# Block inverses of two tiles and both directions in shared banks, paired scan steps, and unread matmuls in the routes

## The chip, the core and the metric

One NeuronCore of one Trainium2 chip runs the whole program. The metric is the device time of one execution in microseconds (us); less is better. The kernel before took 1251.12 us (median of three runs, 1250.53 to 1254.74). The rows below come from one profiled execution of it, which has a time of its own. Everything is f32 or a pair of fp32r numbers (a high and a low part), so that most projections are three matmuls.

## What is computed

Two blocks over 256 tokens of 1024 channels. The first block has two layers, each a mixer and an expert layer (16 experts, 32 tokens each, chosen by the experts). The first layer's mixer is a gated delta rule with four heads in both directions, over the tokens (`lat`) and 256 tokens of context, plus a pooling branch. The second block (a linear recurrence and an attention) is not touched. Of the reference, this is what the change works on:

```python
t_mat = jnp.eye(c) + jnp.where(strict, kk * decay, 0.0) * beta[..., :, None]
u = solve(t_mat, v * beta[..., None])
wk = solve(t_mat, k * (beta * jnp.exp(gam))[..., None])

def advance(s, u_c, wk_c, kd_c, cd_c):
    w = u_c - jnp.einsum('bhck,bhkv->bhcv', wk_c, s)
    return w, cd_c * s + jnp.einsum('bhck,bhcv->bhkv', kd_c, w)

def step(s, inp):
    w, s_new = advance(s, u_c, wk_c, kd_c, cd_c)
    o = qd_c @ s + qk_c @ w
...
aff = jax.nn.softmax(jnp.einsum('bnd,de->bne', h, router), axis=-1)
gate, idx = lax.top_k(aff.transpose(0, 2, 1), cap)
xg = h[bidx, idx]
hid = silu(xg @ w_gate) * (xg @ w_up)
```

## The kernel before

**The first mixer.** The 512 tokens lie in four tiles of 128: tiles 0 and 1 are the tokens, 2 and 3 the context. For each direction `dr` and tile `tt` the kernel needs the inverse of a 128x128 unit triangular matrix for each of four heads. The diagonal 32x32 blocks are solved on VectorE (`diagonal`, unit D), then `inverse` joins them to 64 and 128 with small matmuls: 32x32 (lines 774, 779, 784) and 64x64 (792, 795), all into banks named `lv`. Each small product is evicted (to `H`, `T`, or straight into the matrix) before the next level reads it. The scan steps (`step`, 804 to 852) then run per direction and tile: kS = k S, T = v - decay kS, w = inverse T, then `wd` and dS (new state), and for token tiles the outputs oi and qS. A direction's steps hang on each other through S; the two directions don't. `pairs` lists what is done side by side: (0,2) with (1,3), (0,3) with (1,2), (0,0) with (1,1), (0,1) with (1,0).

In between, the same stage computes `ada` (A0 to A4: rows of the modulation vectors of later layers, 4 x 8 matmuls of 32x512 each, from weights that are loaded for it), `zp` (Z: two halves of the gate and pool projections), and kq (C: scores). Line numbers with a 2 or 3 in the hundreds (`L353` to `L355`) are the projections' helpers.

**What sets the order.** `ORDER["mixer0"]` names the units in order; `trace` calls them one after the other, and a unit that yields is called several times (`each`). From this a scheduler makes each engine's queue, in which it may interleave neighbours; an engine works through its queue in order. PSUM tags share banks: "ps" 2, "ada" 1, "a" 3, "b" 2. Weights are loaded by SyncE's one queue, in program order, into rings of buffers; a load waits until its buffer has been read.

**After the mixer.** A tail normalises the outputs (og, oT) and the pooled part; `residual` multiplies by the output weights; its eight tiles feed `moe` through `tile_done`, which also collects the router's sums and transposes the tokens (`xtok`). Then the route: `lg` (router logits), exponentials (`aff`), a transpose (affT), four rounds of top-8 on VectorE (`cur`), positions (`pos`, posT), the one-hot matrices (`oh`), and `xg`, the gathered tokens, with which the gate and up matmuls (gu, L1122) and the down matmuls (dn, L1148) run on weight tiles wg, wu, wd. The scaled tokens `xn` (ScalarE, L1079) are needed by xg only. The call of `free` opens the ring for the expert weights of the layer.

## Time and profile before

| what | us |
|---|---|
| runs | 1251.12 median, 1250.53 to 1254.74 |
| the profiled execution's own time | 1252.43 |
| its span | 1250.7 |
| busy in the span: TensorE, VectorE, ScalarE, GpSimd | 1094.5, 629.2, 492.8, 68.6 |
| half of the first mixer that holds inverses and steps | 176 to 266 |
| layer 0: last block of expert weights has landed | 524.25 |
| layer 1: affT, posT, first xg begin | 641.58, 647.63, 648.51 |
| layer 1: the chain enters the expert weights | 670.08 |

Three kinds of rows are used. The chain of waits follows the work that ended last back through the span; the table by stretches gives each engine's busy time, the granted TensorE clock (1.00 is 2.4 GHz, 0.50 is 1.2 GHz) and the traffic between two times; the timeline lists an engine's pieces with their start and length. A plain f32 matmul stands in the trace as two instructions, an fp32r one as one, so "x8" of lv or ada are four matmuls. In a timeline a piece's end runs into the next one's start, since matmuls are pipelined; the distance from start to start is what a piece took.

### The profile page before, as it was taken

To read this page: it belongs to the slowest core of one execution; us is meant where nothing else is said; L and a number is where in the kernel's file an instruction comes from. 1 tells how busy PE (TensorE), PEld (TensorE's weight loads), DVE (VectorE), ACT (ScalarE), POOL (GpSimd) and SP (SyncE) were. 2 spreads that over 40 slices of the span, in tenths; PEclk is the share of its full clock that TensorE was granted. 3 is DMA by queue.
4 is the path that set the end of the run, shared out by engine and by line. 5 is a ranking of instruction groups with operands and counts; after the bars stand their busy time and mean duration, and the time that the engine had idled before them with its cause. 6 is when DMAs were issued, how large, how long until landed. Compare 5 with 4: busy or idle time off the path is not lost.

```text
span 1250.7 us, 19471 instructions
## 1 busy us (share of the span) xinstructions
PE 1094.5 (88%) x7728; PEld 741.0 (59%) x7728; DVE 629.2 (50%) x1442; ACT 492.8 (39%) x1035; POOL 68.6 (5%) x118
## 2 busy tenths in 40 slices
PE   5999999989799666799979956668999999999997
PEld 2667656658443120299844411117898699988875
DVE  3548972354321010378631100017887887689875
ACT  4347553243201000255511100006778466566663
POOL 0050000000000000000000000000001100011100
PEclk9999899999799777799979987878999999999999
DMA  9578565579999999998459999994352145433220
GB/s 387 201 271 307 200 265 196 173 270 374 372 422 421 421 422 421 422 420 335 160 223 416 421 421 422 421 421 188 125 187 94 68 151 183 161 136 129 102 102 34
DMA packets 48043, 339.71 MB, mean 272 GB/s; under 512 B 5328, under 2 KB 5584, under 8 KB 7248
## 3 DMA queue, kind: packets, MB, share of 16 engines
q1 hardware_dynamic: 46800, 336.38, 68.4%
q10 hardware_dynamic: 1152, 2.09, 0.5%
q8 instruction: 61, 1.00, 0.3%
q14 instruction: 30, 0.25, 0.1%
HBM read 337.40 MB, written 1.05 MB: 271 GB/s over the span
## 4 chain that ended last, share of the span: by engine, by line
PE 39%; DMA 23%; issue 7%; DVE 5%; ACT 2%; POOL 1%; POOLq 0%; DVEq 0%; SPq 0%; ACTq 0%
DMA w<-wu 8%; DMA w<-wg 8%; DMA w<-wd 6%; PE gu L1122 3%; PE xg L1097 2%; PE sc L344 2%; PE sc L342 2%; PE sc L343 2%; PE qkvg L342 2%; PE qkvg L344 2%; PE qkvg L343 2%; DMA pk<-pk 1%; PE dn L1148 1%; PE res L342 1%; PE res L343 1%
## 5 line engine op out<-in xcount | busy, mean ns | idle before, releaser
L297 DVE TENSOR_TENSOR wl<-w,wh 128x512 fp32r<-128x512 f32 x304 | 208.4, 695 | 82.8 <-ACT wh L211 72.9
L211 ACT ACTIVATE wh<-w 128x512 fp32r<-128x512 f32 x304 | 189.2, 631 | 144.9 <-PE res L343 25.8
L1122 PE MATMUL gu<-w,xg 128*32 128x512 f32 x1024 | 161.0, 729 | 50.9 <-DMA w<-wu 28.1
L1122 PEld LDWEIGHTS gu<-w,xg 128*32 128x32 f32 x1024 | 30.3, 117 | 164.8 <-DMA w<-wu 74.0
L1148 PE MATMUL dn<-w,hidT 128*32 128x512 f32 x512 | 70.4, 652 | 21.7 <-DMA w<-wd 16.1
L1137 DVE TENSOR_TENSOR hid<-hid,gu 128x512 f32<-128x512 f32 x8 | 5.5, 686 | 159.7 <-PE gu L1122 159.7
L211 ACT ACTIVATE y<-dn 128x512 f32<-128x512 f32 x16 | 9.6, 598 | 188.2 <-PE dn L1148 188.2
L232 DVE SCALAR_TENSOR_TENSOR xT<-sc,adac,xT 128x256 f32<-128x256 f32 x64 | 27.9, 480 | 106.4 <-PE sc L1156 106.4
L342 PE MATMUL qkvg<-u_f,wh 128*128 128x272 f32 (+1 forms) x256 | 74.1, 290 | 0.0
L344 PE MATMUL qkvg<-u_f,wl 128*128 128x272 f32 (+1 forms) x256 | 73.2, 286 | 0.0
L343 PE MATMUL qkvg<-u_f,wh 128*128 128x272 f32 (+1 forms) x256 | 72.8, 284 | 0.0
L437 PE MATMUL ada<-w,cs 128*32 128x512 f32 x320 | 54.6, 641 | 1.3 <-DMA w<-ada 1.3
L344 PE MATMUL sc<-hT,wl 128*128 128x258 f32 x192 | 54.7, 285 | 0.9 <-DVE wl L297 0.9
L342 PE MATMUL sc<-hT,wh 128*128 128x258 f32 x192 | 54.6, 284 | 0.2 <-DVE xT L232 0.2
L343 PE MATMUL sc<-hT,wh 128*128 128x258 f32 x192 | 54.2, 282 | 0.0
L1148 PEld LDWEIGHTS dn<-w,hidT 128*32 128x32 f32 x512 | 14.2, 115 | 66.7 <-DMA w<-wd 37.1
L342 PEld LDWEIGHTS qkvg<-u_f,wh 128*128 128x128 f32 x256 | 48.1, 188 | 3.0 <-issue 1.8
L344 PEld LDWEIGHTS qkvg<-u_f,wl 128*128 128x128 f32 x256 | 48.2, 188 | 0.8 <-issue 0.8
L343 PEld LDWEIGHTS qkvg<-u_f,wh 128*128 128x128 f32 x256 | 48.2, 188 | 0.0
L1136 ACT ACTIVATE hid<-gu 128x512 f32<-128x512 f32 x8 | 4.8, 598 | 104.4 <-PE gu L1122 104.4
L1156 PE MATMUL sc<-sg,y 128*128 128x256 f32 x128 | 37.3, 442 | 8.5 <-ACT y L211 8.4
L1156 PEld LDWEIGHTS sc<-sg,y 128*128 128x128 f32 x128 | 26.3, 216 | 25.9 <-ACT y L211 22.2
(613 smaller groups left out, 2624.8 us busy)
## 6 DMA issues: line engine op xcount, KB each, us to landing
w<-wu SPq DMA_DIRECT2D x64, 1024.0 KB, 19.8
w<-wg SPq DMA_DIRECT2D x64, 1024.0 KB, 19.8
w<-wd SPq DMA_DIRECT2D x64, 1024.0 KB, 19.8
w<-ada SPq DMA_DIRECT2D x48, 1024.0 KB, 5.3
w<-f_in SPq DMA_DIRECT2D x16, 1024.0 KB, 4.9
w<-sc_in SPq DMA_DIRECT2D x12, 1024.0 KB, 19.8
w<-e_out SPq DMA_DIRECT2D x8, 1024.0 KB, 5.3
w<-ev_ws SPq DMA_DIRECT2D x6, 1024.0 KB, 6.0
```

Of the source, the lines that this page charges most:

```text
L211: return self.nc.scalar.activation(out, in_, AF.Copy)
L232: return self.nc.vector.scalar_tensor_tensor(out, a, s, b, op0=op0, op1=op1, **kw)
L297: self.nc.vector.tensor_sub(lo, x, hi.bitcast(F32))
L342: mm(out, wh, xh, start=(kt == 0), stop=False)
L343: mm(out, wh, xl, start=False, stop=False)
L344: self.last_mm = mm(out, wl, xh, start=False, stop=(kt == nk - 1)).ins
L437: nc.tensor.matmul(a[32 * q:32 * q + 32, :], self.cs[:, kt, :], w[:, q * 512:(q + 1) * 512], start=(kt == 0), stop=(kt == KT - 1), tile_po ...
L1097: nc.tensor.matmul(a[:, :256], xn[:, i, ft * P:(ft + 1) * P], oh[:, i].rearrange("p e s -> p (e s)"), start=(i == 0), stop=(i == 1))
L1122: nc.tensor.matmul(a[32 * e:32 * e + 32, :], xg[g // 2][:, kt, s:s + 32], w[:, e * 512:(e + 1) * 512], start=(kt == 0), stop=(kt == KT - 1 ...
L1137: v.tensor_mul(hid, hid, pu[1])
L1148: nc.tensor.matmul(a[32 * e:32 * e + 32, :], hT[:, t, 32 * e:32 * e + 32], w[:, e * 512:(e + 1) * 512], start=(t == 0), stop=(t == 3), til ...
L1156: nc.tensor.matmul(a[:, j * 256:(j + 1) * 256], y[:, (2 * f2 + j) * P:(2 * f2 + j + 1) * P], sg[g // 2][:, g % 2], start=True, stop=True)
```

## The change

`inverse(n)` now treats two tiles and both directions at once: n is 0 or 1 (tiles 0 and 1, or 2 and 3), its products of both directions and tiles go into one shared bank for each level, and each eviction takes all of them (or one direction) at once. It yields four times. `step(pair, last)` runs both directions of a pair side by side, operation by operation, and yields twice: once after the state, once after the outputs. `ORDER["mixer0"]` is rewritten for these units: I0 is `inverse(1)` (context), I1 is `inverse(0)`; the gates and decays stand earlier, the ada units later. In the route, `warm(n)` adds n unread f32 matmuls of 128x256 into the "ada" bank: five behind the last `lg`, ten behind affT. The last two `xtok` transposes come behind `lg`, and the `xn` activations behind the exponentials. (`ada_columns` is split out of `ada` without effect; a new `ada_sum` is called by no unit, since ADA_SUM is empty.) In the diff the removed lines of `inverse` and `step`, which stand in the code above, are left out.

```diff
+WARM = 5, 10
+ADA_SUM = ()
...
 ORDER = {
-    "mixer0": "k0 K0 G A0 W0 A1 W1 W0 W1 W1 W1 W0 W0 k1 K1 k2 K2 k3 K3 Q0 R0 R1 R2 R3 v0 V0 v1 V1 v3 V3 v2 V2 Q1 Q2 "
-              "Q3 D A2 A3 I0 I0 I1 I0 I0 I1 U I1 P0 I2 I3 P1 I1 P0 P1 C0 Z I2 C1 P2 Z Z I2 I3 P3 I2 P2 A4 I3 Z I3 "
-              "P3",
+    "mixer0": "k0 G W1 K0 W1 W0 W0 A0 W1 W0 W1 W0 k1 K1 k2 K2 A1 k3 K3 Q0 R0 R1 R2 R3 v0 V0 v1 V1 v3 V3 v2 V2 Q1 Q2 "
+              "Q3 D A2 I0 I1 A3 I0 I0 I0 U P0 P0 I1 A4 P1 Z I1 I1 C1 C0 P1 Z P2 Z Z P2 P3 P3",
...
-        def inverse(pair):
...
+        def inverse(n):
...
+            q4 = lambda q: slice(32 * q, 32 * q + 32)
+            half = lambda i: slice(64 * i, 64 * i + 64)
+            ts = slice(2 * n, 2 * n + 2)
+            dirs = [(AA[0][:, ts], R_[:, 0, ts], RT_[:, 0, ts], 0, 1), (AA[1][:, ts], RT_[:, 1, ts], R_[:, 1, ts], 1, 0)]
+            blocks = [(p, *d, 2 * p + d[3], 2 * p + d[4]) for p in range(2) for d in dirs]
+            th = [(t, h) for t in range(2) for h in range(4)]
+            T = gw.tile([P, 2, 4, 64], F32, tag="YT64", name="YT64", bufs=1)
+            H = gw.tile([P, 2, 4, 32], F32, tag="H32", name="H32", bufs=1)
+            a, a2 = (self.ps("lv", t).rearrange("p (x t h c) -> p x t h c", x=2, t=2, h=4) for t in "ba")
+            for p, A, Yi, YT, R, C, r, c in blocks:
+                for t, h in th:
+                    mm(a[q4(c), 0, t, h], A[q4(r), t, h, q4(c)], YT[q4(r), t, h], start=True, stop=True,
+                       tile_position=(32 * r, 32 * c))
+            self.copy(H, a[:, 0], "act")
+            g.memset(T, 0.0)
+            for Z, Yi, YT, R, C in dirs:
+                for q in (2 * R, 2 * R + 1):
+                    self.copy(T[q4(q), :, :, q4(q % 2)], YT[q4(q)])
+            yield
+            for p, A, Yi, YT, R, C, r, c in blocks:
+                for t, h in th:
+                    mm(a[q4(r), 1, t, h], H[q4(c), t, h], Yi[q4(c), t, h], start=True, stop=True,
+                       tile_position=(32 * c, 32 * r))
+            for p, A, Yi, YT, R, C, r, c in blocks:
+                if p == R:
...
+            for p, Z, Yi, YT, R, C, r, c in blocks:
+                nc.scalar.activation(Z[q4(r), :, :, q4(c)], a[q4(r), 1], AF.Copy, scale=-1.0)
+                if p == R:
+                    v.tensor_scalar(T[q4(c), :, :, q4(r % 2)], a2[q4(c), 0], -1.0, None, op0=OP.mult)
+            for Z, Yi, YT, R, C in dirs:
                 for q in range(4):
...
+                    self.copy(Z[q4(q), :, :, q4(q)], Yi[q4(q)])
+            yield
+            H = gw.tile([P, 2, 4, 64], F32, tag="H64", name="H64", bufs=1)
+            b, b2 = (self.ps("lv", t).rearrange("p (t h c) -> p t h c", t=2, h=4) for t in "bb")
+            for A, _, _, R, C in dirs:
+                for t, h in th:
+                    mm(b[half(C), t, h], A[half(R), t, h, half(C)], T[half(R), t, h], start=True, stop=True,
+                       tile_position=(64 * R, 64 * C))
+            self.copy(H, b, "act")
+            yield
+            for Z, _, _, R, C in dirs:
+                for t, h in th:
+                    mm(b2[half(R), t, h], H[half(C), t, h], Z[half(C), t, h, half(C)], start=True, stop=True,
+                       tile_position=(64 * C, 64 * R))
+            for Z, _, _, R, C in dirs:
+                v.tensor_scalar(Z[half(R), :, :, half(C)], b2[half(R)], -1.0, None, op0=OP.mult)
+            yield
...
+        def step(pair, last):
...
             hd = lambda t, h: t[:, h * P:(h + 1) * P]
...
+            tk = lambda tt: slice(tt * P, (tt + 1) * P)
+            mm = lambda out, x, y: nc.tensor.matmul(out, x, y, start=True, stop=True)
+            T1, w, wr, old = {}, {}, {}, list(S)
+            for dr, tt in pair:
+                if S[dr] is None:
+                    T1[dr] = vtok[:, tt, :]
+                    continue
                 a = self.ps("kS", "a")
                 for h in range(4):
...
+                    mm(hd(a, h), kT[:, h, tk(tt)], hd(S[dr], h))
+                T1[dr] = sw.tile([P, 512], F32, tag="T1", name="T1")
                 for h in range(4):
...
+                    self.stt(hd(T1[dr], h), hd(a, h), neg[:, dr, tt, h:h + 1], hd(vtok[:, tt, :], h), OP.mult, OP.add)
+            for dr, tt in pair:
+                w[dr] = b = self.ps("w", "a")
+                for h in range(4):
+                    mm(hd(b, h), AA[dr][:, tt, h], hd(T1[dr], h))
+            wd = {}
+            for dr, tt in pair if not last else ():
+                wd[dr] = sw.tile([P, 512], F32, tag="wd", name="wd")
+                for h in range(4):
+                    nc.scalar.activation(hd(wd[dr], h), hd(w[dr], h), AF.Copy, scale=bkd[:, dr, tt, h:h + 1])
+            for dr, tt in pair if pair[0][1] < 2 else ():
+                wr[dr] = sw.tile([P, 512], F32, tag="wr", name="wr")
+                for h in range(4):
+                    nc.scalar.activation(hd(wr[dr], h), hd(w[dr], h), AF.Copy, scale=beta[:, tt, 4 * dr + h:4 * dr + h + 1])
             if not last:
...
+                for dr, tt in pair:
+                    c = self.ps("dS", "a")
                     for h in range(4):
...
+                        mm(hd(c, h), hd(ktok[:, tt, :], h), hd(wd[dr], h))
+                    Sn = sw.tile([P, 512], F32, tag=f"S{dr}", name="S")
+                    if S[dr] is None:
+                        v.tensor_copy(Sn, c)
+                    else:
+                        for h in range(4):
+                            self.stt(hd(Sn, h), hd(S[dr], h), ec[:, dr, 2, tt, h:h + 1], hd(c, h), OP.mult, OP.add)
+                    S[dr] = Sn
+            yield
+            for dr, tt in pair if pair[0][1] < 2 else ():
                 e = self.ps("oi", "a")
                 for h in range(4):
...
+                    mm(hd(e, h), KQ[dr][:, tt, h], hd(wr[dr], h))
                 f = self.ps("qS", "a")
                 for h in range(4):
...
+                    mm(hd(f, h), qT[:, h, tk(tt)], hd(old[dr], h))
                 O = oacc[tt]
                 of = O.rearrange("p h d -> p (h d)")
                 if not done[tt]:
                     v.tensor_add(of, of, e)
                 for h in range(4):
                     self.stt(O[:, h], hd(f, h), ec[:, dr, 0, tt, h:h + 1], O[:, h], OP.mult, OP.add)
...
+            yield
         pairs = [[(0, 2), (1, 3)], [(0, 3), (1, 2)], [(0, 0), (1, 1)], [(0, 1), (1, 0)]]
...
-        def steps(i):
-            for dr, tt in pairs[i]:
-                step(dr, tt, i == 3)
-                yield
...
-            units[f"I{h}"] = each(inverse(pairs[h]), 4)
-            units[f"P{h}"] = each(steps(h), 2)
+            units[f"P{h}"] = each(step(pairs[h], h == 3), 2)
...
+        for n in range(2):
+            units[f"I{n}"] = each(inverse(1 - n), 4)
...
+    def warm(self, n):
+        x = self.xT.rearrange("p k t -> p (k t)")
+        a = self.ps("warm", "ada")
+        for i in range(n):
+            self.nc.tensor.matmul(a[:, :256], self.ident, x[:, :256], start=True, stop=True)
...
+                        self.last_lg = nc.tensor.matmul(lg[:, 64 * i + 32 * n + m:][:, :m], (x, sq)[n][:, t],
+                                                        (Rs[:, kt], self.ones)[n][:, :m], start=True, stop=True).ins
+            with self.tc.issue_after(self.last_lg) if kt == KT - 1 else ExitStack():
+                for i in range(2):
+                    pe = self.tp(xt[i][kt // 4][:, (kt % 4) * P:(kt % 4 + 1) * P], x[:, i * P:(i + 1) * P])
             return pe
...
+        with self.tc.issue_after(self.last_lg):
+            self.warm(WARM[0])
...
-            nc.scalar.activation(aff[:, i], aff[:, i], AF.Exp, bias=mx[:, i:i + 1], accum_out=ex[:, i:i + 1])
+            e = nc.scalar.activation(aff[:, i], aff[:, i], AF.Exp, bias=mx[:, i:i + 1], accum_out=ex[:, i:i + 1])
...
         for i in range(2):
-            self.tp(at[:16, i * P:(i + 1) * P], aff[:, i])
+            at_ins = self.tp(at[:16, i * P:(i + 1) * P], aff[:, i]).ins
+        with self.tc.issue_after(at_ins):
+            self.warm(WARM[1])
...
         xn = wk.tile([P, 2, D], F32, name="xn")
-        for b in range(2):
-            for i in range(2):
-                nc.scalar.activation(xn[:, i, 512 * b:512 * b + 512], xt[i][b], AF.Copy, scale=rs[:, i:i + 1])
+        with self.tc.issue_after(e.ins):
+            for b in range(2):
+                for i in range(2):
+                    nc.scalar.activation(xn[:, i, 512 * b:512 * b + 512], xt[i][b], AF.Copy, scale=rs[:, i:i + 1])
```

TensorE, start of the inverses in the first mixer; `lv` are the small products (R and RT the solved diagonal blocks, A the matrix, H an evicted product), `zp` the gate projection; a row is a run of matmuls of one kind, and the line numbers of the change are its own. Before:

```order
L355 MATMUL zp<-wh,hl_291 128x512
L774 MATMUL lv<-RT,A 32x32 x4
L353 MATMUL zp<-wh,hl_290 128x512
L354 MATMUL zp<-wl,hl_290 128x512
L774 MATMUL lv<-RT,A 32x32 x4
L355 MATMUL zp<-wh,hl_291 128x512
L353 MATMUL zp<-wh,hl_290 128x512
L779 MATMUL lv<-R,H_1882 32x32 x4
```

The same place in the changed kernel:

```order
L795 MATMUL lv<-RT,A 32x32 x8
L795 MATMUL lv<-R,A 32x32 x8
L795 MATMUL lv<-RT,A 32x32 x8
L795 MATMUL lv<-R,A 32x32 x8
L805 MATMUL lv<-R,H_1833 32x32 x8
L805 MATMUL lv<-RT,H_1833 32x32 x8
L805 MATMUL lv<-R,H_1833 32x32 x8
L805 MATMUL lv<-RT,H_1833 32x32 x8
L810 MATMUL lv<-H_1833,R 32x32 x8
L810 MATMUL lv<-H_1833,RT 32x32 x8
L357 MATMUL zp<-wh,hl_291 128x512
```

Small products that stood in fours between projections now stand in one run: eight rows of eight at the first level (the last four of them stand above), then six rows that read H.

TensorE, scan steps, near the end of the ada work. Before:

```order
L437 MATMUL ada<-w,cs 32x512
L818 MATMUL w<-T_2331,A 128x128 x4
L792 MATMUL lv<-YT_2454,A 64x64 x4
L825 MATMUL dS<-wd,ktok 128x128
L437 MATMUL ada<-w,cs 32x512
L825 MATMUL dS<-wd,ktok 128x128
L437 MATMUL ada<-w,cs 32x512
L825 MATMUL dS<-wd,ktok 128x128
L437 MATMUL ada<-w,cs 32x512
L825 MATMUL dS<-wd,ktok 128x128
L437 MATMUL ada<-w,cs 32x512
L838 MATMUL oi<-w__2356,KQ 128x128 x4
```

The changed kernel:

```order
L439 MATMUL ada<-w,cs 32x512 x4
L845 MATMUL kS<-S,kT 128x128 x8
L845 MATMUL w<-T_2430,A 128x128 x2
L439 MATMUL ada<-w,cs 32x512 x4
L845 MATMUL w<-T_2430,A 128x128 x2
L845 MATMUL w<-T_2440,A 128x128 x4
L845 MATMUL dS<-wd,ktok 128x128 x4
L439 MATMUL ada<-w,cs 32x512 x4
L357 MATMUL zp<-wh,hl_291 128x512
```

The single ada and dS matmuls that took turns stand in fours, and kS and w of both directions follow each other.

TensorE, the route of layer 0, from the last router sums to the first gate matmuls. Before:

```order
L204 MATMUL xtok<-ident,xT 128x128 x2
L1029 MATMUL lg<-sel_92,qs 128x16 x2
L1009 MATMUL lg<-Rs,xT 128x16 x2
L1009 MATMUL lg<-ones,sq 128x1 x2
L204 MATMUL affT<-ident,aff 16x128 x2
L204 MATMUL posT<-ident,pos 128x16 x2
L1097 MATMUL xg<-oh,xn 128x256 x3
L1122 MATMUL gu<-w,xg 32x512 x4
L1097 MATMUL xg<-oh,xn 128x256 x3
L1122 MATMUL gu<-w,xg 32x512 x8
```

The changed kernel:

```order
L1059 MATMUL lg<-Rs,xT 128x16 x2
L1059 MATMUL lg<-ones,sq 128x1 x2
L206 MATMUL xtok<-ident,xT 128x128 x2
L1017 MATMUL warm<-xT,ident 128x256 x5
L206 MATMUL affT<-ident,aff 16x128 x2
L1017 MATMUL warm<-xT,ident 128x256 x10
L206 MATMUL posT<-ident,pos 128x16 x2
L1153 MATMUL xg<-oh,xn 128x256 x4
L1178 MATMUL gu<-w,xg 32x512 x8
L1153 MATMUL xg<-oh,xn 128x256 x4
```

The transposes moved behind lg, the unread matmuls stand ahead of affT and posT, and xg and gu take turns in larger groups.

## Rows read from the trace of the kernel before

**Rows 1.** The page: its span, and the chain of waits by line.
```profile
span 1250.7 us, 19471 instructions
...
DMA w<-wu 8%; DMA w<-wg 8%; DMA w<-wd 6%; PE gu L1122 3%; PE xg L1097 2%; PE sc L344 2%; PE sc L342 2%; PE sc L343 2%; PE qkvg L342 2%; PE qkvg L344 2%; PE qkvg L343 2%; DMA pk<-pk 1%; PE dn L1148 1%; PE res L342 1%; PE res L343 1%
```

**Rows 2.** By stretches: stretch, length, busy PE PEld DVE ACT POOL, clock, DMA share, GB/s.
```profile
176.00:266.00 90.00, 90.00 (x833) 58.69 (x832) 31.64 (x101) 32.15 (x104) 1.84 (x6) 0.98 0.55 188
405.00:524.00 119.00, 82.83 (x444) 18.96 (x432) 11.66 (x27) 6.64 (x14) 0.00 (x0) 0.76 1.01 422
```

**Rows 3.** The chain in order of time, expert layers: start, us, what.
```profile
404.91 19.81 DMA w<-wg
424.78 19.86 DMA w<-wu
444.70 19.82 DMA w<-wd
...
504.37 19.84 DMA w<-wd
...
670.08 14.82 DMA w<-wg
```

**Rows 4.** Timeline of TensorE: start, us, engine, line, op, out<-in, instructions.
```profile
183.93 0.43 PE L774 MATMUL lv<-RT,A 32*32 32x32 f32 x8
184.29 0.50 PE L353 MATMUL zp<-wh,hl 128*128 128x512 f32 x1
...
184.96 0.34 PE L774 MATMUL lv<-RT,A 32*32 32x32 f32 x5
...
185.48 0.49 PE L818 MATMUL w<-vtok,A 128*128 128x128 f32 x2
...
193.34 1.07 PE L437 MATMUL ada<-w,cs 128*32 128x512 f32 x8
194.34 0.96 PE L792 MATMUL lv<-YT,A 64*64 64x64 f32 x16
195.23 0.71 PE L812 MATMUL kS<-S,kT 128*128 128x128 f32 x4
...
228.44 1.05 PE L437 MATMUL ada<-w,cs 128*32 128x512 f32 x2
229.41 1.16 PE L818 MATMUL w<-T,A 128*128 128x128 f32 x8
230.50 0.68 PE L792 MATMUL lv<-YT,A 64*64 64x64 f32 x8
231.11 0.49 PE L825 MATMUL dS<-wd,ktok 128*128 128x128 f32 x2
231.53 1.04 PE L437 MATMUL ada<-w,cs 128*32 128x512 f32 x2
```

**Rows 5.** By stretches, two neighbouring ones in the inverses (columns as in Rows 2).
```profile
183.20:186.60 3.40, 3.40 (x57) 2.60 (x54) 1.09 (x2) 1.04 (x4) 0.00 (x0) 1.00 0.61 193
186.60:190.00 3.40, 3.40 (x28) 1.51 (x27) 0.00 (x0) 0.30 (x2) 0.00 (x0) 0.50 0.93 328
```

**Rows 6.** Groups by line and shape, VectorE, 175 to 275: busy, mean ns; idle before.
```profile
L232 DVE SCALAR_TENSOR_TENSOR T<-kS,neg,vtok 128x128 f32<-128x128 f32 x24 | 6.8, 345 | 3.4 <-PE kS L812 3.4
```

**Rows 7.** Layer 1's route: the chain's xn piece, then TensorE's timeline, idle in brackets.
```profile
639.68 0.69 ACT xn L1079
...
641.58 0.59 PE L204 MATMUL affT<-ident,aff 128*16 128x128 f32 x2 [3.18 <-ACT xn L1079]
647.63 0.36 PE L204 MATMUL posT<-ident,pos 16*128 16x16 f32 x2 [5.47 <-DVE pos L1070]
648.51 2.93 PE L1097 MATMUL xg<-oh,xn 128*128 128x256 f32 x6 [0.52 <-DVE oh L1090]
651.37 1.93 PE L1122 MATMUL gu<-w,xg 128*32 128x512 f32 x8
653.23 2.05 PE L1097 MATMUL xg<-oh,xn 128*128 128x256 f32 x6
...
660.84 1.99 PE L1097 MATMUL xg<-oh,xn 128*128 128x256 f32 x8
662.76 1.93 PE L1122 MATMUL gu<-w,xg 128*32 128x512 f32 x16
```

**Rows 8.** By stretches, layer 0 as its first gate matmuls run (columns as in Rows 2).
```profile
332.00:340.00 8.00, 8.00 (x50) 3.32 (x46) 1.09 (x2) 1.13 (x2) 0.00 (x0) 0.91 0.92 320
```

More of the change, by code (lines that the diff above doesn't have):

```diff
@@ new lines, in inverse @@
+            for Z, Yi, YT, R, C in dirs:
[9 more added lines that the diff above has]
+                    for t, h in th:
+                        mm(a2[q4(c), 0, t, h], Yi[q4(c), t, h], H[q4(c), t, h], start=True, stop=True,
+                           tile_position=(32 * c, 32 * c))
@@ L850, in step @@
                     self.stt(O[:, h], hd(f, h), ec[:, dr, 0, tt, h:h + 1], O[:, h], OP.mult, OP.add)
-            if not last:
-                S[dr] = Sn
+            yield
         pairs = [[(0, 2), (1, 3)], [(0, 3), (1, 2)], [(0, 0), (1, 1)], [(0, 1), (1, 0)]]
```

101 lines of the change are left out of this document (24 added, 77 removed).

## The prediction

> **What bounds the kernel now.** I read first the page's chain of waits: waits for expert weights (wu, wg, wd) are its largest items [rows 1]. Cut to its two expert layers, the chain shows where they rule: from 404.9 us every piece is a block of eight weight tiles that takes 19.8 us, and in the second layer the same begins at 670.1 [rows 3]. Between them the DMA moves 422 GB/s without a gap [rows 2]. So a layer's end is the time of its first loads plus its megabytes, and whatever moves the first loads moves the end by as much. In layer 0 the loads past the first tiles open when the residual's last matmuls are read, so they hang on the first mixer's end; in layer 1 they hang on the first gate matmuls, which free weight slots.
>
> Next I read the first mixer's second half, 176 to 266 us, in the table by stretches. TensorE is marked busy all 90 us, while VectorE and ScalarE have some 32 us each [rows 2]. The bound is the length of TensorE's own program there. It is not the work of its arithmetic alone: the single pieces [rows 4] show that a matmul group pays an entrance each time TensorE changes kind. I take start to next start:
> - ada: eight instructions (four matmuls, which lie side by side in the array) take 1.00 us from 193.34 to 194.34, two take 0.97 from 228.44 to 229.41. The price is per visit, whatever is in it.
> - 32x32 lv: eight alone 0.36 (183.93), sixteen in two neighbouring groups 0.52 (184.96 to 185.48). So 0.02 an instruction and 0.20 a visit.
> - 64x64 lv: eight 0.61 (230.50), sixteen 0.89 (194.34). So 0.035 each, 0.33 a visit.
> - 128x128: eight 1.09 (229.41), two 0.42 (231.11). So 0.11 each, 0.20 a visit.
>
> **The inverses and scan steps.** From the first lv to the last qS both built programs hold the same 160 small, 64 middle and 131 or 132 full matmuls and 64 of ada; zp has 45 before and 49 after. The work is not cut. What is cut is visits (a visit: a run of one kind): 139 before, 49 after. By kind: ada 23 to 16, small lv 35 to 4, middle lv 17 to 7, full 40 to 15, zp 24 to 7. Priced: 7 x 0.98 = 6.9; 31 x 0.20 = 6.2; 10 x 0.33 = 3.3; 25 x 0.20 = 5.0; together 21.4 us. zp's fewer visits I set against its four more matmuls: nothing. The merged evictions (104 small ones become 44) count nothing by themselves, since VectorE and ScalarE are two thirds idle here [rows 2]; the two memsets that replace eight are on GpSimd, which idles.
>
> Three things are to be taken off.
> - New waits. Before, each eviction had another tile's lv or a zp under it. After, where only one pair of steps is in flight, matmuls of both directions stand for the same kind of eviction. An operation on one head takes 0.345 us [rows 6], four heads 1.4. In the new order nearly every handover still has ada, lv or kq behind it; the last pair (kS, T, w, wr, oi) has none. Three handovers x 1.4 = 4.1. The bounds are nothing and twelve handovers (three in each of four pairs), 16.6. I take 4, since the order shows cover at most of them.
> - The clock. In 183.2 to 186.6 TensorE is busy without a gap, 57 instructions, mostly small lv and w, at 1.00 (2.4 GHz); in the next 3.4 us the granted clock is 0.50 (1.2 GHz) [rows 5]. The new program has longer runs of nothing but 32x32 matmuls. One such spell costs half its length, 1.7; before has one, after perhaps two, so 1.7 more (bounds 0 and 5.1).
> - The tail. Both tokens' tiles finish together after the last pair, so one more normalisation stands ahead of the residual: four heads x 0.345 = 1.4.
> 21.4 - 4.1 - 1.7 - 1.4 = 14.2 us that the residual starts, and so the loads and the end of layer 0 come, earlier. Two ada loads wait in the queue behind an output-weight load, which needs zp's last split; in the new order that split can follow the third zp group, well ahead of those ada matmuls, with oi, qS and forty zp between, so I cost it at nothing (without that cover it would be two loads, each a little over 19.8 / 8 = 2.5 us).
> The rest of the reordered list (gates first, ada later) keeps the counts ahead of the first lv nearly equal (zp 47 for 51): nothing, with 2 us either way.
>
> On the clock the Trainium skill says otherwise: "TensorE: Matmul & The Clock Gate", Part 1, has the throttle follow how busy TensorE has been, so that a busy one keeps the full clock. By it no spell is added and the sum is 1.7 better; the trace disagrees, 0.50 right after a stretch without idle [rows 5].
>
> **The routes.** In layer 1 [rows 7]: xn (0.69) stands on ScalarE ahead of the exponentials, and the change puts it behind: 0.7 less. The two transposes moved behind lg and five unread matmuls must fit ahead of affT. An unread 128x256 matmul costs as one of xg, 1.92 / 4 = 0.48 at full clock (660.84 to 662.76), so 2.4 in a gap that was 3.18 and is now about 2.5: it fits within 0.3, set against the transposes' own gain. Ten more are 4.8 in a gap of 5.47: they fit. If they hold the clock, xg and gu, which ran at half (2.86 for three matmuls, 1.86 for one tile's gu), take 4 x 0.48 + 0.93 = 2.85 where 648.51 to 653.23 is 4.7. The first slot is free 0.7 + 1.9 = 2.6 earlier, the next ones still more, since one tile's gu now follows the other: I take 3.0 (bounds 0.7 and 4.5). That passes whole into a stretch that DMA bounds.
> In layer 0 the same happens, but the loads were running meanwhile. Only their hole can close: 332 to 340 us at 320 GB/s against 422 [rows 2, 8] is 8 x (1 - 320/422) = 1.9 us. I take 1.9 (bounds 0 and 2.5).
>
> **The sum.** 14.2 + 1.9 + 3.0 = 19.1 us. The profiled execution took 1252.4 (span 1250.7 [rows 1]); it would take 1233.3. The median of the runs shown, 1251.1, is 1.3 lower, so 1232.
>
> **The rivals.**
> - Everything overlaps: no new waits, no clock spell, and big packs run closer than 0.02 each. 21.4 + 5 to 7 gives 1223. For it: evictions have idle engines. Against: the last pair has no cover.
> - The stage's gain is eaten: about twelve handovers at 1.4, 16.6, and two clock spells leave the residual where it was; only the routes gain, 4.9: 1246. For it: the filler that lay between has been packed together. Against: ada, kq and lv still stand between most steps.
> - Slower: the steps of both directions go through the evicting engine as one burst of eight heads, 8 x 0.345 = 2.8, and TensorE, which works in order, stands for the whole of it at all twelve handovers: 33 us against 21.4 + 4.9 gained, with the tail 1259. It decides from about 2.1 us a handover. Against: the second direction's matmuls are ready while the first is evicted.
> - The inverses' neighbours stand apart. Sixteen small lv took 0.52 and not twice 0.36 where two tiles with two banks of their own met [rows 4]; now both directions write into one bank, which before never shows. If such neighbours do not run into each other, the 6.2 and the 3.3 us of the inverses are not gained: 1232 + 9.5 is 1241.5. For it: nothing in the trace excludes it. Against: within one group, too, matmuls into one bank follow at 0.02 to 0.03 an instruction. (The Trainium skill has this as a rule: "TensorEngine Tiling (Array Packing)", Gotcha 1, says that different row tiles cannot use one PSUM bank at the same time. No row of before shows such a bank.)
> - The warming does not warm: the ten unread matmuls run at half clock, 9.6 in a gap of 5.5, and posT comes 4.1 late in both layers. That leaves 14.2 less 3.4 in each, 7.4: 1244. Against: TensorE is at full clock until lg.
>
> **How the numbers follow.** Forecast 0.66 (1224 to 1240), everything overlaps 0.10, neighbours apart 0.08, gain eaten 0.09, warming fails 0.04, slower 0.03. A measurement of this kernel can tell about 0.3%, 3.8 us, from no change. A fifth of gain eaten ends within that, hence faster 0.94, same 0.03, slower 0.03. For 8 in 10 the range takes the forecast's own, the neighbours apart, the nearer part of everything overlaps (0.06) and the nearest of gain eaten: 1221 to 1242.
>
> **What would show it.** The first-mixer stretch from first lv to last qS should be some 83 us instead of 97, with idle before oi and og but little elsewhere; ada in 16 visits of 1.0. xg in both layers should start at full clock, and in layer 1 the loads should resume near 650.5 less the shift of the rest. The blocks of 19.8 us must be unchanged. I am wrong if TensorE shows idle at lv behind ScalarE's H, if the clock is 0.5 through most of the inverses, or if the residual starts early but the loads do not follow.

## The result, and the profile after

The changed kernel took 1238.33 us (median of four runs, 1233.16 to 1244.99), the kernel before 1252.93 (four runs): a ratio of 0.9889, 95% interval 0.9857 to 0.9922. Seven further runs, taken with the experiments, had a median of 1243.37 (1237.44 to 1244.71) against 1251.44 for the kernel before: 0.9917 (0.9884 to 0.9951). So it is faster, by 0.8 to 1.1%. Its eleven runs lie 11.8 us apart; eleven runs of the kernel before, taken beside e9_interleave_apart, lie 12.5 apart (1248.28 to 1260.77). The profiled execution took 1233.16 us, with a span of 1231.4: it is the fastest of the eleven, which has to be kept in mind when its rows are set against those of before.

The page of the changed kernel, its span and the chain of waits by line:

```profile
span 1231.4 us, 19493 instructions
...
DMA w<-wu 10%; DMA w<-wd 8%; DMA w<-wg 6%; PE ada L439 3%; PE gu L1178 3%; PE sc L346 2%; PE sc L345 2%; PE sc L344 2%; DMA pk<-pk 2%; PE qkvg L344 2%; PE qkvg L346 2%; PE qkvg L345 2%; DVE wl L299 1%; PE res L345 1%; PE res L344 1%
```

The chain still ends in the same loads [rows 1]; ada is new in it. Its pieces in order of time (start, us, what):

```profile
467.76 19.81 DMA w<-wu
487.63 19.84 DMA w<-wd
507.51 1.11 PE dn L1204 x8
...
787.77 19.82 DMA w<-wd
807.61 18.12 DMA pk<-pk
826.41 0.57 PE meta L1325 x16
```

A block of eight weight tiles takes 19.8 us as before [rows 3]; the last one of layer 0 has landed at 507.5 in place of 524.2.

Where the time went, by points that both timelines of TensorE show (first lv, end of the last qS, taken as the start of what follows it, first res, first lg of a layer, first xg, end of the last dn, first meta of the second block), in us from one point to the next:

| stretch | before | changed, first profile | changed, second profile |
|---|---|---|---|
| first lv to last qS | 97.4 | 79.7 | 79.6 |
| last qS to first res (tail) | 8.8 | 10.0 | 10.0 |
| first res to lg, layer 0 | 34.6 | 36.0 | 36.2 |
| lg to xg, layer 0 | 12.3 | 12.6 | 12.6 |
| xg to last dn, layer 0 | 196.4 | 194.2 | 194.2 |
| lg to xg, layer 1 | 12.2 | 12.6 | 12.6 |
| xg to last dn, layer 1 | 196.7 | 194.2 | 194.4 |
| first meta to the end of the span | 405.2 | 405.0 | 407.9 |

And the stage from the first lv to the last qS by kind, each piece from its start to the next start, idle time taken out, summed over the timeline (us / visits):

| kind | before | changed, first profile | predicted change | measured |
|---|---|---|---|---|
| ada | 23.6 / 23 | 16.8 / 16 | -6.9 | -6.8 |
| lv 32x32 | 13.5 / 35 | 9.9 / 4 | -6.2 | -3.6 |
| lv 64x64 | 9.6 / 17 | 8.4 / 7 | -3.3 | -1.2 |
| kS, w, dS, oi, qS | 31.2 / 49 | 26.7 / 28 | -5.0 | -4.5 |
| zp | 14.3 / 24 | 13.2 / 7 | 0 | -1.1 |
| idle | 1.4 | 0.5 | +4.1 | -0.9 |

(Here w, dS and so on count as kinds of their own, so that the visits of full matmuls are more than the prediction's 40 and 15.) TensorE's timeline of the changed kernel shows the prices (start, us, engine, line, op, out<-in, shapes, instructions):

```profile
201.13 0.59 PE L810 MATMUL lv<-H,R 32*32 32x32 f32 x13
...
201.65 0.57 PE L810 MATMUL lv<-H,RT 32*32 32x32 f32 x13
202.15 1.38 PE L845 MATMUL kS<-S,kT 128*128 128x128 f32 x10
203.46 1.07 PE L439 MATMUL ada<-w,cs 128*32 128x512 f32 x8
204.46 0.94 PE L845 MATMUL kS<-S,kT 128*128 128x128 f32 x6
...
211.08 1.90 PE L824 MATMUL lv<-YT,A 64*64 64x64 f32 x32
212.91 1.16 PE L756 MATMUL kq<-qT,kT 128*128 128x128 f32 x8
```

An ada visit is 1.00 from 203.46 to 204.46, as in [rows 4]. A run of 32 small products takes 1.02 (201.13 to 202.15), 0.032 each, entrance included; 32 middle ones take 1.83 (211.08 to 212.91), 0.057 each, where sixteen had taken 0.89 [rows 4]: the pace by instruction is as bad as before, so that fewer visits brought little here.

The clock is the second thing. By stretches (length, busy PE PEld DVE ACT POOL, granted clock, DMA share, GB/s), first the changed kernel's inverses, then its tail:

```profile
176.00:182.00 6.00, 5.99 (x210) 5.68 (x208) 4.05 (x12) 4.33 (x12) 0.00 (x0) 0.94 0.63 265
182.00:184.00 2.00, 1.48 (x17) 1.42 (x18) 0.39 (x1) 0.46 (x2) 0.00 (x0) 0.50 0.00 0
184.00:190.00 6.00, 6.00 (x69) 3.52 (x69) 1.80 (x4) 2.63 (x6) 0.53 (x1) 0.66 0.33 97
190.00:196.00 6.00, 6.00 (x95) 4.48 (x96) 1.95 (x4) 2.33 (x6) 0.00 (x0) 1.00 0.72 255
```

```profile
256.00:260.00 4.00, 2.07 (x14) 1.48 (x13) 2.69 (x10) 1.76 (x5) 1.01 (x1) 0.97 0.22 53
260.00:270.00 10.00, 8.45 (x32) 6.43 (x32) 5.51 (x16) 3.75 (x8) 1.01 (x1) 0.50 1.00 421
270.00:274.00 4.00, 4.00 (x35) 3.77 (x35) 2.54 (x5) 1.95 (x4) 0.00 (x0) 1.00 0.49 205
```

After 5 us of nothing but small products, in which TensorE is marked busy without a gap, the clock is at 0.50 (1.2 GHz) until about 188.1: a spell of (1 - 0.94) x 2 x 6 + 2 + 0.34 x 2 x 6 = 6.8 us at half clock, where before had 3.4 [rows 5]. And a second spell of 10 us begins in the tail, behind a stretch in which TensorE is busy half the time, and covers the first res matmuls. The kernel before had none there; its tail:

```profile
273.00:282.00 9.00, 5.42 (x28) 3.18 (x27) 6.05 (x18) 5.24 (x12) 1.01 (x1) 1.00 0.98 407
```

TensorE is idle in it for about as long (3.7 us before, 3.3 in the changed kernel), so idle time in the tail alone does not tell the two apart.

### The profile page after: what moved, and what is told of

Its sections match the earlier page's. It is cut to its first block, busy times and chain, and to the rows that moved or that the text cites. A ratio compares the mean times of both kernels' runs of the same rounds, so it can differ in the third digit from the quotient of the medians.

```text
span 1231.4 us, 19493 instructions
## 1 busy us (share of the span) xinstructions
PE 1087.1 (88%) x7788; PEld 743.5 (60%) x7788; DVE 627.6 (51%) x1422; ACT 482.3 (39%) x995; POOL 64.5 (5%) x112
## 4 chain that ended last, share of the span: by engine, by line
PE 53%; DMA 27%; DVE 8%; issue 7%; ACT 3%; POOL 2%; POOLq 0%; SPq 0%; DVEq 0%; ACTq 0%
DMA w<-wu 10%; DMA w<-wd 8%; DMA w<-wg 6%; PE ada L439 3%; PE gu L1178 3%; PE sc L346 2%; PE sc L345 2%; PE sc L344 2%; DMA pk<-pk 2%; PE qkvg L344 2%; PE qkvg L346 2%; PE qkvg L345 2%; DVE wl L299 1%; PE res L345 1%; PE res L344 1%
## 5 line engine op out<-in xcount | busy, mean ns | idle before, releaser
L1178 PEld LDWEIGHTS gu<-w,xg 128*32 128x32 f32 x1024 | 26.9, 118 | 168.7 <-DMA w<-wu 75.3
L1204 PE MATMUL dn<-w,hidT 128*32 128x512 f32 x512 | 69.3, 638 | 24.9 <-DMA w<-wd 19.1
L346 PEld LDWEIGHTS qkvg<-u_f,wl 128*128 128x128 f32 x256 | 48.3, 189 | 0.8 <-issue 0.8
L439 PE MATMUL ada<-w,cs 128*32 128x512 f32 x320 | 46.4, 630 | 0.0
## 6 DMA issues: line engine op xcount, KB each, us to landing
w<-wu SPq DMA_DIRECT2D x64, 1024.0 KB, 19.8
w<-wg SPq DMA_DIRECT2D x64, 1024.0 KB, 19.8
w<-wd SPq DMA_DIRECT2D x64, 1024.0 KB, 19.8
w<-sc_in SPq DMA_DIRECT2D x12, 1024.0 KB, 19.8
```

The source lines that it names most:

```text
L346: self.last_mm = mm(out, wl, xh, start=False, stop=(kt == nk - 1)).ins
L439: nc.tensor.matmul(a[32 * q:32 * q + 32, :], self.cs[:, kt, :], w[:, q * 512:(q + 1) * 512], start=(kt == 0), stop=(kt == KT - 1), tile_po ...
L1178: nc.tensor.matmul(a[32 * e:32 * e + 32, :], xg[g // 2][:, kt, s:s + 32], w[:, e * 512:(e + 1) * 512], start=(kt == 0), stop=(kt == KT - 1 ...
L1204: nc.tensor.matmul(a[32 * e:32 * e + 32, :], hT[:, t, 32 * e:32 * e + 32], w[:, e * 512:(e + 1) * 512], start=(t == 0), stop=(t == 3), til ...
```

## The experiments

Each kernel was timed beside the kernel before on one chip. "Stage" is first lv to the end of the last qS.

| run | median us (range) | ratio to before, 95% | stage | half clock, 176 to 210 | tail | res to lg |
|---|---|---|---|---|---|---|
| changed, first profile | 1238.3 (1233.2 to 1245.0) | 0.9889 (0.9857 to 0.9922) | 79.7 | 6.8 | 10.0 | 36.0 |
| e1_after_again | 1243.4 (1237.4 to 1244.7) | 0.9917 (0.9884 to 0.9951) | 79.6 | 6.8 | 10.0 | 36.2 |
| e2_mixer_only | 1243.9 (1236.2 to 1248.9) | 0.9917 (0.9890 to 0.9945) | 85.7 | 20.5 | 9.6 | 36.8 |
| e3_routes_only | 1251.3 (1248.3 to 1256.1) | 0.9992 (0.9971 to 1.0012) | 96.2 | 0 | 8.8 | 34.6 |
| e4_nowarm | 1241.6 (1236.1 to 1243.5) | 0.9909 (0.9873 to 0.9945) | 79.8 | 6.8 | 10.0 | 36.3 |
| e5_interleave | 1236.3 (1231.9 to 1236.8) | 0.9857 (0.9838 to 0.9876) | 76.4 | 6.8 | 10.0 | 36.2 |
| e6_lv_warm | 1242.8 (1241.7 to 1246.6) | 0.9918 (0.9901 to 0.9936) | 85.3 | 0 | 10.0 | 36.9 |
| e7_tail_warm | 1239.4 (1233.6 to 1246.6) | 0.9886 (0.9855 to 0.9917) | 82.6 | 13.7 | 13.8 | 34.4 |
| e8_steps_apart | 1247.8 (1241.4 to 1251.8) | 0.9950 (0.9927 to 0.9973) | 93.7 | 20.5 | 8.0 | 37.0 |
| e9_interleave_apart | 1229.2 (1225.2 to 1236.4) | 0.9801 (0.9767 to 0.9836) | 74.2 | 3.4 | 10.0 | 37.1 |
| e10_apart | 1242.0 (1238.1 to 1245.3) | 0.9902 (0.9867 to 0.9937) | 79.8 | 6.8 | 10.0 | 36.2 |

### The spread of the changed kernel, and the routes

e1_after_again is the changed kernel itself.

> The changed kernel once more, for the spread of its runs (1233 to 1245 us so far) and a second profile. If the spread comes from the granted clock in stretches that TensorE bounds, runs with a lower mean clock are longer by about the time that the clock explains (0.933 went with 1231.4 us of span, 0.925 with 1243.2) and the stage from the first lv to the last qS is again 79.7 us. Rival: the spread comes from the new program itself, its waits in the first mixer; then that stage differs between this profile and the first one by several us.

Its stage is 79.6 us again and the 4.4 us that this profile is longer lie elsewhere (2.9 of them in the second block, which no edit touches). So these two profiles don't show what the slower runs, at 1243 to 1245, do. The next kernel's gives a hint. e2_mixer_only takes the routes' edits back:

```diff
-WARM = 5, 10
+WARM = 0, 0
...
-            with self.tc.issue_after(self.last_lg) if kt == KT - 1 else ExitStack():
+            with ExitStack():
...
-        with self.tc.issue_after(e.ins):
+        with ExitStack():
```

> The changed first mixer with the routes as before (no unread matmuls, xtok and xn where they were). Sum of the prediction: the mixer carries 14.2 of 19.1 us, so about 4.9 us over the changed kernel; the trace of the changed kernel says 1.9 in layer 0 and some 2.3 in layer 1, so 4. Rival, the routes are hidden behind the loads: equal to the changed kernel. Affinity transpose to first xg as before, xg at half clock in both layers.

Its first mixer is the changed kernel's, matmul for matmul, yet its stage took 85.7 us in the profiled execution. The stretches of e2_mixer_only:

```profile
182.00:184.00 2.00, 1.28 (x38) 1.17 (x35) 0.00 (x0) 0.75 (x2) 0.00 (x0) 0.68 0.00 0
184.00:190.00 6.00, 6.00 (x45) 3.53 (x44) 2.19 (x4) 2.36 (x5) 0.00 (x0) 0.50 0.16 27
190.00:196.00 6.00, 6.00 (x62) 4.04 (x61) 0.57 (x2) 1.42 (x3) 0.52 (x1) 0.50 0.36 150
196.00:202.00 6.00, 6.00 (x63) 5.51 (x62) 1.38 (x2) 1.50 (x4) 0.00 (x0) 0.50 0.53 178
202.00:208.00 6.00, 6.00 (x46) 3.59 (x44) 0.69 (x1) 2.17 (x8) 0.00 (x0) 0.90 0.53 175
```

The same spell that ended at 188.1 in the changed kernel goes on to 203.2: 20.5 us at half clock instead of 6.8, and the stage is 6.0 us longer, 0.44 us for each us of spell. e7_tail_warm below, whose edits too come behind this stage only, lies between: a spell of 13.7 us and a stage of 82.6. One stretch of program thus has a spell of several lengths: in the changed kernel, e1_after_again, e4_nowarm, e7_tail_warm and e2_mixer_only TensorE's matmuls are the same, in the same order, up to the last qS, and the spell is 6.8 (three times), 13.7 and 20.5. Its length is worth up to 6 us, half of the 12 us over which the changed kernel's runs are spread; that its slowest runs are those with a long spell fits the mean clock of their records (0.921 to 0.929 for the five runs at 1243 and more, 0.930 to 0.934 for four of the six faster ones, 0.922 and 0.929 for the other two), but no profile of such a run of the changed kernel itself was taken, so this is argued, not shown. Other pieces vary too: the second block took 2.9 us longer in the second profile, and the first lv comes at 176.2 to 178.7 us in those five profiles (181.4 in e10_apart, with the same matmuls up to it).

e3_routes_only is the reverse: the first mixer as before, `moe` and `warm` as in the change (no other edit).

> The first mixer as before with the changed routes. If the two parts add, it is 4 to 5 us (0.3 to 0.4%) under the kernel before, with xg x8 at 1.9 us in both layers and the logits at the same time as before. Rival, everything of the gain is the mixer's: no difference.

e4_nowarm leaves the unread matmuls out and keeps xtok and xn in their new places (WARM = 0, 0).

> The changed kernel without the unread matmuls (the last xtok transposes and the xn activations stay in their new places). If the unread matmuls are what makes xg and gu start at full clock, xg and gu run at half clock again for some 4 us in both layers and nearly all of the routes' 4 us is lost; affT comes about 0.6 us earlier after lg than in the changed kernel. Rival, the new places alone are worth it: within 1 us of the changed kernel.

By the medians the routes are worth nothing that these runs can tell: 1251.3 against 1251.4 for the routes alone (interval: 3.6 us gained to 1.5 lost), and e2_mixer_only (1243.9) and e4_nowarm (1241.6) lie within 3 us of the median of the changed kernel's eleven runs, 1240.9, with ranges of 7 to 13 us. The profiles are finer, since they let the routes' stretches be taken apart from the mixer's. From the first lg to the end of the last dn, layer 0 takes 206.7 and 206.8 us in the two profiles of the changed kernel, 208.7 before, 207.6 in e2_mixer_only, 207.7 in e4_nowarm; layer 1 takes 206.8 and 207.0, against 208.9, 208.0 and 209.0. So beside e2_mixer_only, which has the same mixer, the routes bring 0.9 and 1.2 us, and beside e4_nowarm 1.0 and 2.2: 2 to 3 together. The unread matmuls bring it: without them, xtok and xn in their new places bring nothing that shows. e3_routes_only, in its one profile, gains 0.2 in layer 0 and 2.2 in layer 1; its stretch between the layers, first ssq to lg, takes 118.7 us where it took 117.3, but the other profiles have 116.1 to 119.1 there, so this need not be the routes' doing. How the matmuls do it, in layer 1 of the changed kernel (timeline of TensorE, idle time in brackets), and below, of e3_routes_only:

```profile
621.40 4.01 PE L1017 MATMUL warm<-xT,ident 128*128 128x256 f32 x10
625.25 0.38 PE L206 MATMUL affT<-ident,aff 128*16 128x128 f32 x2
625.47 4.58 PE L1017 MATMUL warm<-xT,ident 128*128 128x256 f32 x20
631.01 0.29 PE L206 MATMUL posT<-ident,pos 16*128 16x16 f32 x2 [0.96 <-DVE pos L1125]
631.91 1.96 PE L1153 MATMUL xg<-oh,xn 128*128 128x256 f32 x8 [0.61 <-DVE oh L1146]
633.80 1.92 PE L1178 MATMUL gu<-w,xg 128*32 128x512 f32 x16
```

```profile
635.20 2.32 PE L975 MATMUL warm<-xT,ident 128*128 128x256 f32 x10
638.27 0.38 PE L205 MATMUL affT<-ident,aff 128*16 128x128 f32 x2 [0.74 <-ACT xn L1093]
```

The five ahead of affT take 2.32 us where the clock is up, and fit; in both layers of both profiles of the changed kernel the clock has already gone down, they take 3.85 and affT waits for them. Of the 18 layers profiled with these matmuls they fit in 6, both of e9_interleave_apart among them. The ten behind it run at full clock (4.58, with 0.96 idle left), and xg and gu start at full clock: 1.89 for eight xg where six took 2.86 [rows 7].

### The small products: paces, places and the clock

e5_interleave turns the loops of `inverse` inside out, at all five places, like this:

```diff
-            for p, A, Yi, YT, R, C, r, c in blocks:
-                for t, h in th:
+            for t, h in th:
+                for p, A, Yi, YT, R, C, r, c in blocks:
                     mm(a[q4(c), 0, t, h], A[q4(r), t, h, q4(c)], YT[q4(r), t, h], start=True, stop=True,
                        tile_position=(32 * r, 32 * c))
```

> The changed kernel, with the small products of one level issued in turn over their places in the array (for each tile and head all four 32x32 places, or both 64x64 places) instead of place after place; same matmuls, same banks. In the changed kernel 32x32 products follow each other every 0.025 us and 64x64 every 0.055 us. Theory A, that is the pace of one place, and products in different places run side by side, also into one bank: the 9.9 us of small and 8.4 us of middle products fall by about half, the stage from first lv to last qS is some 72 us in place of 79.6, and the half-clock spell after the first run of lv shrinks; 6 to 9 us faster. Theory B, products in different places into one bank don't overlap: nothing moves (within 1 us).

Theory A holds for the products and fails for the stage: small products take 4.6 us in place of 9.9, middle ones 5.8 in place of 8.4, the sum 7.9 less; but idle time rises from 0.5 to 5.1 us, and the stage falls by 3.3. Timeline of TensorE in e5_interleave, idle time in brackets:

```profile
179.71 0.21 PE L805 MATMUL lv<-R,H 32*32 32x32 f32 x1 [0.91 <-ACT H L213]
...
183.49 0.26 PE L810 MATMUL lv<-H,R 32*32 32x32 f32 x1 [2.80 <-issue]
...
209.20 1.15 PE L824 MATMUL lv<-YT,A 64*64 64x64 f32 x32
210.28 1.16 PE L756 MATMUL kq<-qT,kT 128*128 128x128 f32 x8
...
234.40 1.06 PE L439 MATMUL ada<-w,cs 128*32 128x512 f32 x8 [1.39 <-DMA w<-ada]
```

32 middle products take 1.08 (209.20 to 210.28) instead of 1.83: 0.034 each, the pace that the prediction had read from a pair of tiles. So products in the two places do run side by side, also where both write into one bank; it is the order of issue that kept them apart. (The Trainium skill, "TensorEngine Tiling (Array Packing)", Gotcha 1, says that different row tiles cannot use one PSUM bank at the same time. Here products of different row tiles into one bank overlap, in 1.08 us in place of 1.83.) The gain uncovers what it had hidden: the second level now waits for its eviction (0.91), and TensorE stands 2.80 us in the middle of a run of small products, for "issue", that is, for nothing that it waits for in the profile. The changed kernel has 0.53 us of it at the same place, ahead of the 209th instruction of the small products. The trace has something beside it: a DMA queue marked "instruction" brings blocks of 16 KB (61 in the whole program, 1.00 MB). Timeline of the changed kernel, then that queue in e5_interleave between 180 and 184 us:

```profile
182.52 1.05 PE L810 MATMUL lv<-H,RT 32*32 32x32 f32 x16 [0.53 <-issue]
```

```profile
q8 instruction: 1, 0.02, 1.5%
```

The block of e5_interleave begins at 181.0 and has landed at 181.9, and TensorE goes on at 183.5; in the changed kernel it has landed at 181.0, and TensorE goes on at 182.5. All seven profiles with such a standstill (0.35 to 2.80 us, one in each) have it there, and it ends 1.2 to 1.6 us after a block has landed. So TensorE has probably run ahead of its own instructions; no run tested that. This version has a median of 1236.3, against 1238.3 and 1243.4 in the two sets of the changed kernel, 2 to 7 us less where 6 to 9 were expected.

e6_lv_warm puts one unread matmul behind each block of the first two levels of the first inverse:

```diff
+                if n == 1:
+                    with tc.issue_after(i):
+                        self.warm(1, "a")
```

> The changed kernel with eight unread 128x256 matmuls, one behind each block of sixteen instructions of small products in the first inverse (8 x 0.48 = 3.8 us more work there). Theory: the half-clock spell of 7 us (first two profiles) to 20 us (the one of the mixer alone) follows the unbroken run of 32x32 products, in which TensorE is marked busy. Broken up, the clock stays at 1.00 in 176 to 196 us, the stage is 79.6 + 3.8 - 3.4 = 80 us in every run, and the runs spread less than the 1233 to 1245 us of the changed kernel; median about 1239. Rival: the clock falls for another reason (the stretch of low load on VectorE's solve ahead of it): the spell stays, and the time is 3.8 us longer.

Stretches of e6_lv_warm:

```profile
182.00:190.00 8.00, 8.00 (x146) 5.42 (x145) 0.60 (x2) 0.38 (x1) 0.00 (x0) 1.00 0.34 104
190.00:196.00 6.00, 6.00 (x86) 4.03 (x86) 1.73 (x4) 3.11 (x7) 0.00 (x0) 1.00 0.65 228
```

The clock stays up, the only profile with the new mixer in which it does, so the spell follows the unbroken run and not the solve ahead of it, which is unchanged, and TensorE being marked busy doesn't hold the clock. But the stage is 85.3 and not 80. Its timeline shows the price of a visit once more:

```profile
178.63 0.69 PE L795 MATMUL lv<-RT,A 32*32 32x32 f32 x16
179.25 0.70 PE L1023 MATMUL warm<-xT,ident 128*128 128x256 f32 x2
179.88 0.69 PE L795 MATMUL lv<-R,A 32*32 32x32 f32 x16
180.50 0.70 PE L1023 MATMUL warm<-xT,ident 128*128 128x256 f32 x2
```

Sixteen small instructions take 0.62 here; where they follow their like, 192 take 4.88 (176.18 to 181.06 in the changed kernel), 0.41 for sixteen. Coming back to the small ones thus costs 0.21 each time, and the unread matmul itself takes 0.62 in place of the 0.48 that I had counted. Eight of them add 8 x (0.62 + 0.21) = 6.6 us and save a spell worth 3; of the 2 us that are left, half goes with the w and middle products, which fell into 27 visits (16) and take 17.1 us (16.1). A remedy for the clock that costs more than the clock.

e9_interleave_apart and e10_apart break the run up without extra work, by the order list; e9 has the loops of e5, e10 those of the change:

```diff
-              "Q3 D A2 I0 I1 A3 I0 I0 I0 U P0 P0 I1 A4 P1 Z I1 I1 C1 C0 P1 Z P2 Z Z P2 P3 P3",
+              "Q3 D A2 I0 A3 I0 I0 I0 U P0 I1 P0 I1 A4 P1 Z I1 I1 C1 C0 P1 Z P2 Z Z P2 P3 P3",
```

> Products in turn over their places (as in the interleaved kernel), and the second inverse's first level called after the first scan step, not right behind the first inverse's: the first unbroken run is 80 small matmuls in place of 112, and other work stands between the levels. Theory: the 2.8 us that the interleaved kernel stands inside that run with nothing to wait for, the 0.9 us in front of the second level and part of the half-clock spell (6.8 us, costing 3) come from the unbroken run; broken, the stage falls from 76.5 to some 71 to 73 us and the time is 3 to 5 us under the interleaved kernel's 1236.3. Rival: the half clock follows the solve ahead of the run, in any order, and the stage stays near 76.

> The same order list with the products place after place, as in the changed kernel. Theory: if the spell of 7 to 20 us follows the length of the unbroken run of small products, it is shorter (0 to 3.4 us) and the same in every run: the stage is 76 to 78 us in place of 79.6 to 85.7, the spread of the runs shrinks from 12 us to under 6, and the median is 1236 to 1238. Rival: the small run takes 5 us here as before and the spell comes as in the changed kernel; then 1240, and the stage 80 us or more.

Stretches of e9_interleave_apart, then of e10_apart:

```profile
176.00:182.00 6.00, 3.92 (x169) 2.77 (x169) 5.41 (x15) 5.86 (x15) 0.00 (x0) 1.00 0.84 352
182.00:184.00 2.00, 2.00 (x10) 0.22 (x9) 1.70 (x4) 1.49 (x4) 0.00 (x0) 0.65 0.00 0
184.00:190.00 6.00, 6.00 (x135) 4.30 (x132) 1.91 (x5) 2.06 (x4) 0.53 (x1) 0.83 0.70 199
```

```profile
186.00:190.00 4.00, 4.00 (x36) 1.78 (x31) 2.13 (x4) 1.81 (x5) 0.00 (x0) 0.60 0.00 0
190.00:196.00 6.00, 6.00 (x89) 4.52 (x88) 1.68 (x4) 2.06 (x4) 0.53 (x1) 0.98 0.75 214
196.00:204.00 8.00, 8.00 (x84) 5.11 (x80) 1.65 (x3) 2.18 (x8) 0.00 (x0) 0.79 0.94 361
```

e9's stage does what was expected, somewhat less: no 2.80 us of standing (its waits are 1.6 us for an ada load, 1.0 for the eviction of H, 1.0 for zp), one spell of 3.4, and 74.2 us where 71 to 73 were expected. The median is 1229.2: 24.1 us under the kernel before, ratio 0.9801 (0.9767 to 0.9836), the best of all kernels here. Of the 7.1 us by which it lies under e5_interleave's median the stage explains 2.3; the profiled spans, 1229.6 and 1230.1, don't show the rest. For e10 the theory fails: split in two, the run gives two spells of 3.4 us each, 6.8 together, the stage is 79.8 and the median 1242.0. The runs, 1238.1 to 1245.3, spread over 7 us and not 12, which six runs don't make a finding. Moving the small products apart was worth something here only after their time had been cut.

### The tail, and the scan steps

e7_tail_warm puts two unread matmuls behind each second pooling product and behind each group of output transposes:

```diff
+            with tc.issue_after(last):
+                self.warm(2)
```

> The changed kernel with twelve unread 128x256 matmuls in the tail of the first mixer, two behind each pooling product and two behind each group of output transposes. In the changed kernel the tail (last qS to first res) takes 9.97 us where it took 8.84, and res starts at half clock until some 4 us later. Theory: the spell comes from the idle tail; filled, the clock stays at 1.00, res runs at 0.11 us a matmul from its start, and the logits come 1.5 to 2.5 us earlier after the last qS (46.0 us in the changed kernel, 43.4 before); 2 us faster. Rival, the unread matmuls stand in the way: 12 x 0.48 = 5.8 us of work in some 3.9 us of idle time, up to 2 us slower.

The rival holds. Stretches of e7_tail_warm:

```profile
261.00:266.00 5.00, 4.50 (x28) 3.92 (x27) 3.68 (x13) 2.27 (x6) 1.01 (x1) 1.00 0.39 110
266.00:272.00 6.00, 3.67 (x15) 2.91 (x14) 3.48 (x12) 2.38 (x5) 1.01 (x1) 0.80 1.00 421
272.00:276.00 4.00, 3.60 (x16) 2.40 (x15) 1.17 (x2) 0.69 (x1) 0.00 (x0) 0.88 1.01 428
```

The spell shrinks to 0.20 x 2 x 6 + 0.12 x 2 x 4 = 3.4 us and res to lg falls to 34.4 us, the length of before; but the tail grows from 10.0 to 13.8, so the logits come 48.3 us behind the last qS in place of 46.0. The median doesn't show the 2 us.

e8_steps_apart has `step` of the kernel before (direction after direction, two calls a pair) in the changed kernel, and the same order list.

> The changed kernel with the scan steps of the kernel before (direction after direction), the new inverses and the same order list. In the changed kernel w, dS, kS, oi and qS take 26.7 us where they took 31.2. Theory of visits: the steps fall apart into more visits, those products take some 30 us again, and the stage is 2 to 4 us longer (82 to 83.5); 3 us slower. Rival, the pairing adds waits that cost as much as it saves: within 1 us.

Its profiled execution has the longest spell (20.5 us), so it is set against e2_mixer_only, which has the same; and its stage holds pooling products that elsewhere come behind the last qS, so the stretch taken is from the first lv to the first res: 101.7 us against 95.3. The pairing is worth 6.3 us, twice what was expected, and the median, 1247.8, agrees with 4 to 7. The products kS to qS fall into 45 visits (28 in e2_mixer_only) and take 29.5 us (27.1); 2.9 us more are idle. In this order list, which was written for paired steps, the pairing thus doesn't add waits, it removes some.

## Why the prediction came out right, and where it was off

**The median was in the range, and the sum was a few us too good.** Forecast were 1232 us and 19.1 us of gain; measured were 1238.3 and 14.6 in the first set. In the second set they were 1243.4, which lies above the range that ended at 1242, and 8.1. In the first profile the span fell by 19.3 us (1250.7 to 1231.4), and its parts are those of the sum: lg of layer 0 comes 14.8 us earlier (forecast 14.2), layer 0 brings 1.9 more (1.9), layer 1 2.1 (3.0), the second block 0.2. That agreement is partly luck, since it is the fastest of eleven executions and since errors inside cancel. The stage fell by 17.7 where its terms make 15.6 (21.4 - 4.1 - 1.7; the "some 83 us" given as a sign count the tail in, without it they make 81.8, and 79.7 was measured), and the clock behind the tail took 1.4 back.

**Which terms held.** Fewer visits at a fixed price: ada -6.8 (forecast -6.9), full matmuls -4.5 (-5.0). The tail: +1.1 (+1.4). Layer 0's hole in the loads: 1.9, though e2_mixer_only, without the new routes, has 1.1 of it. The blocks of 19.8 us are unchanged, and a layer's end moves with its first loads.

**Small and middle products were mis-sized:** -4.8 in place of -9.5. The slopes, 0.02 and 0.035 an instruction, came from groups in which two tiles with banks of their own met. In the changed kernel sixteen in one place follow each other at 0.025 and, the middle ones, at up to 0.057. Some 1.4 of the 4.7 us that are missing are half clock and belong to the clock's term: 32 small products took 1.91 us in the spell (181.06 to 183.50 without the standstill) where 1.02 is their time, 32 middle ones 2.33 (186.95 to 189.28) where 1.83. That is the rival of the neighbours that stand apart, at about half of its price, and for another reason than the one given with it: e5_interleave shows that one bank for both directions is no hindrance, and that the order of issue is.

**New waits were not paid.** Forecast +4.1, measured 0.9 less idle time than before. Both directions side by side, with ada, kq and zp between, cover the evictions; e8_steps_apart shows the pairing to be worth 6.3 us. The rival in which the gain is eaten by handovers thus falls, and the slower one with it. The waits do come where the products are made faster (5.1 us in e5_interleave).

**The clock was counted too small.** One more spell of 3.4 us (1.7) is what the best profiles show, 6.8 against 3.4. But the spell has other lengths in other executions of the same stretch, up to 20.5 us, 6.0 more. The sentence that named this as the way to be wrong, half clock through the inverses, is what e2_mixer_only's profile shows. And a second spell, in the tail, was not in the sum: res to lg takes 36.0 us in place of 34.6. The prediction's statement on the Trainium skill's rule ("TensorE: Matmul & The Clock Gate", Part 1) stands: a TensorE marked busy lost its clock, and e6_lv_warm, where larger matmuls break the run, kept it.

**The routes** were forecast at 4.9 and bring 2 to 3 in the profiles. The step that failed is that the first five unread matmuls fit ahead of affT. They were priced at full clock (2.4 us) and take 3.85 in the changed kernel's layers, so that xg starts 0.3 later after lg where 0.7 earlier was in the sum (in the 6 layers in which they do fit it starts some 0.4 earlier, 11.8 us after lg); the rest, xg at full clock, is as forecast (1.89 us for eight instructions, 1.92 in the sum). The rival in which the ten run at half clock falls. In the medians this gain is below what can be told.

**What stays open:** what sets a spell's length from one execution to the next, how much of the changed kernel's spread it makes, what starts the spell in the tail, and whether it is for its instructions that TensorE stands inside a run of small products.

## What to carry to other kernels

On an engine that changes between kinds of work, count visits before instructions: one price per visit explained ada and the full matmuls to 10%. Small matmuls in different places of the array ran side by side only where neighbours in the queue had different places; turning two loops inside out cut their time from 18.3 to 10.4 us, and with the order list around them it gained about as much again as the whole change (a ratio of 0.9801 to the kernel before, against 0.9889 and 0.9917). And a price read from one pair of neighbours should be read again at the number of neighbours that the new program has.
